# One layer of a hybrid attention trunk: a new order at the front, two weight sums on VectorE, a new place for the operands of two products, another term order in ff2, and other engines for the last rows

## The chip, the cores and the metric

The kernel runs on one core of one Trainium2 chip. The metric is the device time of one execution in microseconds (us), the median of several runs. Engines are named as the profile names them: PE (TensorE, matmuls), PEld (its weight loads), DVE (VectorE), ACT (ScalarE), POOL (GpSimd) and SP (SyncE, which issues DMAs here).

## The reference

Inputs are float32, the batch is 1, the sequence 512 rows, the model width 1024. RMSNorm divides a row by its root mean square and multiplies by a gain.

```python
u = rms_norm(h, g_mix)
z = u @ w_in                       # q, k, v of two attentions, forget logits, 2 x 1024 gates
y_a = sliding_window_attention(...) @ w_br_swa     # window 128, ALiBi, sinks
y_b = forgetting_attention(...) @ w_br_fox         # causal, decay bias from cumsum(log f)
mixed = sigmoid(gates[0]) * y_a + sigmoid(gates[1]) * y_b
h = h + mixed @ w_mix_out
u = rms_norm(h, g_mlp)
h = h + square(relu(u @ w_ff1)) @ w_ff2            # 1024 -> 4096 -> 1024
h = h + sigmoid(rms_norm(h, g_ple) @ w_ple_gate) * (p @ w_ple_proj)
out = rms_norm(h, g_final)
```

## The kernel before

**Three products for one.** Every matmul operand is kept as a high part (fp32r, cast by ACT) and a low part (what is left, subtracted by DVE). The helper `hi_lo` (L70 ACT, L71 DVE) splits activations; `emit_split` (L324 ACT, L325 DVE) splits weights into tiles named u0h, u0l, u1h and so on, the number counting the weight units in the order of use. A product is three matmuls: high by high, high by low, low by high. Four slots hold the high and four the low parts of weights, so a split waits until PE has ended the product that used the slot before.

**Rows.** The 512 rows are four blocks (tb) of 128. At the front each block is squared and summed (`square1`, DVE L435 for one half, ACT L432 for the other), POOL takes the root (L359, L362), DVE scales (`scale1`, L447), PE transposes in two halves of four 128x128 pieces (`to_uT`, L379), and `hi_lo` splits each half. The first products on it are those for v (`v_mm`, L467), for which `split_v` (L453, L454) splits eight blocks of weights.

**Seven products for eight.** ff1, ff2 and part of the gates use a scheme of the Strassen kind: a 2 x 2 block product is made from seven products of sums of blocks, numbered 1 to 7. ff1 products (`win_mm`, L910, 24 matmuls of 256 columns) are named ('f1', g) with the output bank x, y or z; ff2 products (`s2_mm`, L1309, 12 matmuls of 512 columns) are named s_. For ff1 the sums of activations are made once, in the mix stage (`put`), and kept split in `u2` and `at_ff`: products 1, 2, 4 and 6 have their operands in `u2`, one behind the other; the last three of them lie 48 words (`SHIFT`) off. For ff2, o is the squared ReLU of a product, split anew in each repetition. Sums of weights are made by `sum_source`: by an accumulating DMA that POOL issues (L298) or by DVE (L296).

**MLP in four repetitions.** The order within a repetition is a1 b1 a2 a5 b5 b2 a6 b6 a7 a3 b7 b3 A1 a4 b4 B1 A2 A5 B5 B2 A6 B6 A3 A7 B7 B3 A4 B4, with a, b ff1 of the even and the odd group, A, B ff2 of them. So products 1 of ff1 come directly behind the repetition before, and products 4 directly behind ff2's A1.

**What sets the order.** PE and POOL run in the order in which the code is written. ACT, DVE and SP are ordered by hand at the front, around the mix stage's end with the first steps of the first repetition, and in the last rows; elsewhere a scheduler orders them from dependencies and estimated times.

**The last rows.** `gate_piece` computes the last row block's gate in two pieces of 256 columns; `merge` (L1398 ACT, L1399 and L1400 DVE) applies a piece to h; `merge_ssq` (L1404 ACT) squares and sums it; POOL adds the sums (L1452) and takes the root (L1454); DVE and ACT scale (L1456 to L1462) and SP issues two stores (L1457, L1463).

## Time and profile before

| | before |
|---|---|
| median of 3 runs | 721.55 us (721.35 to 722.12) |
| the profiled execution's own time | 721.84 us |
| its span in the profile | 720.1 us |
| mean granted TensorE clock | 0.997 |
| one repetition of the MLP | about 77 us |

The span is what the profile sees of the execution; 1.74 us lie around it. A row of the timeline gives start and length in us, engine, line, operation, what it writes and reads, and in brackets how long the engine stood idle just before and what ended that. A row of the chain of waits gives start, length and what the time went to. A row of the stretches gives start:end, length, then busy time and count of instructions of PE, PEld, DVE, ACT and POOL, the granted clock, the DMA share and GB/s. Matmuls that follow each other without a stop overlap, so the pace is read from one start to the next, not from a row's length.

### The profile page before, as it was taken

To read this page: it belongs to the slowest core of one execution; us is meant where nothing else is said; L and a number is where in the kernel's file an instruction comes from. 1 tells how busy PE (TensorE), PEld (TensorE's weight loads), DVE (VectorE), ACT (ScalarE), POOL (GpSimd) and SP (SyncE) were. 2 spreads that over 40 slices of the span, in tenths; PEclk is the share of its full clock that TensorE was granted. 3 is DMA by queue.
4 is the path that set the end of the run, shared out by engine and by line. 5 is a ranking of instruction groups with operands and counts; after the bars stand their busy time and mean duration, and the time that the engine had idled before them with its cause. 6 is when DMAs were issued, how large, how long until landed. Compare 5 with 4: busy or idle time off the path is not lost.

```text
span 720.1 us, 11455 instructions
## 1 busy us (share of the span) xinstructions
PE 705.6 (98%) x4229; PEld 626.6 (87%) x4229; DVE 531.5 (74%) x900; ACT 449.4 (62%) x836; POOL 87.6 (12%) x127
## 2 busy tenths in 40 slices
PE   7999999999999999999999999999999999999995
PEld 6988888888888998888899789988999889988884
DVE  5567888877696556545879985899679966997564
ACT  5547888779863553344777646874578546866452
POOL 1011211100001200002410102010300020010101
PEclk9999999999999999999999999999999999999998
DMA  9256456670364894450995598739994689079002
GB/s 290 65 155 159 109 136 154 150 197 1 118 206 116 152 339 162 160 173 11 252 220 202 105 285 168 235 87 254 190 259 113 157 234 227 31 147 349 1 30 87
DMA packets 74055, 116.72 MB, mean 162 GB/s; under 512 B 6664, under 2 KB 44048, under 8 KB 74000
## 3 DMA queue, kind: packets, MB, share of 16 engines
q1 hardware_dynamic: 65792, 86.38, 37.9%
q0 software_dynamic: 8064, 29.36, 22.2%
q8 instruction: 33, 0.54, 0.3%
q10 hardware_dynamic: 144, 0.26, 0.1%
q14 instruction: 22, 0.18, 0.1%
HBM read 72.93 MB, written 4.19 MB: 107 GB/s over the span
## 4 chain that ended last, share of the span: by engine, by line
PE 85%; DVE 9%; ACT 2%; issue 2%; DMA 1%; POOL 0%; POOLq 0%; DVEq 0%; ACTq 0%
PE pf L74 5%; PE pf L76 5%; PE pf L75 5%; PE s_6x L1309 3%; PE s_4x L1309 3%; PE s_0x L1309 3%; PE s_2x L1309 3%; PE h_sc L752 2%; PE h_pv L822 2%; PE h_tr L810 2%; PE psy L75 2%; PE psy L76 2%; PE psy L74 2%; PE psm L76 2%; PE psm L75 2%; PE psm L74 2%
## 5 line engine op out<-in xcount | busy, mean ns | idle before, releaser
L298 POOL DMA_DIRECT2D wq<-wq x26 | 23.6, 942 | 174.9 <-DVE u154l L325 25.9
L770 ACT ACTIVATE s<-s,h_nm 128x128 f32<-128x128 f32 (+1 forms) x64 | 32.6, 512 | 5.9 <-DVE h_nm L763 5.1
L359 POOL TENSOR_SCALAR n_ms<-acc 128x1 f32<-128x1 f32 x15 | 6.3, 419 | 164.8 <-ACT junk L1075 100.4
L71 DVE TENSOR_TENSOR h_ptl<-h_tr,h_pth 128x512 fp32r<-128x512 f32 (+2 forms) x40 | 22.9, 604 | 3.9 <-ACT h_pth L70 3.6
L467 PE MATMUL va<-wv_h,u 128*128 128x320 f32 x64 | 20.1, 319 | 0.8 <-ACT u L70 0.7
L70 ACT CAST h_pth<-h_tr 128x512 fp32r<-128x512 f32 (+2 forms) x40 | 19.4, 523 | 1.8 <-PE h_tr L810 1.4
L70 ACT CAST u<-n_tr 128x512 fp32r<-128x512 f32 x22 | 12.2, 586 | 13.1 <-PE n_tr L1123 5.9
L810 PE MATMUL h_tr<-ident,s 128*128 128x128 f32 x136 | 19.6, 277 | 0.2
L467 PE MATMUL vb<-wv_h,u 128*128 128x328 f32 x64 | 19.6, 313 | 0.0
L298 POOL DMA_DIRECT2D wgw<-wgw x8 | 7.1, 970 | 101.9 <-DVE u25l L325 77.7
L71 DVE TENSOR_TENSOR u<-n_tr,u 128x512 fp32r<-128x512 f32 x22 | 14.6, 685 | 6.5 <-ACT u L70 6.5
L1075 ACT ACTIVATE junk<-h_sb 128x512 f32<-128x512 f32 x16 | 10.1, 630 | 12.3 <-DVE h_sb L1065 9.8
L822 PE MATMUL h_pv<-h_pth,v 128*128 128x256 f32 (+1 forms) x64 | 17.3, 291 | 0.0
L822 PE MATMUL h_pv<-h_ptl,v 128*128 128x256 f32 (+1 forms) x64 | 16.9, 305 | 0.3 <-DVE h_ptl L71 0.3
L810 PEld LDWEIGHTS h_tr<-ident,s 128*128 128x128 f32 x136 | 15.0, 141 | 2.0 <-ACT s L790 0.5
L1399 DVE TENSOR_TENSOR sgp<-sgp,pp 128x512 f32<-128x512 f32 (+1 forms) x9 | 5.7, 633 | 14.6 <-ACT sgp L1398 14.6
L1065 DVE TENSOR_TENSOR h_sb<-psm,h_sb 128x512 f32<-128x512 f32 x8 | 5.5, 689 | 14.3 <-PE psm L76 14.3
L790 ACT ACTIVATE s<-s,h_rec 128x128 f32<-128x128 f32 (+2 forms) x32 | 14.2, 482 | 2.3 <-DVE h_rec L784 2.3
L832 DVE TENSOR_TENSOR h_ao<-h_pv,h_ao 64x512 f32<-64x512 f32 x16 | 10.9, 681 | 6.1 <-ACT h_ao L831 5.8
L758 DVE CUSTOM_DVE_ANT_0 s<-h_sc,causal 128x128 f32<-128x128 f32 (+3 forms) x32 | 13.8, 482 | 0.3 <-PE h_sc L752 0.3
L784 DVE RECIPROCAL h_rec<-h_den 128x4 f32<-128x4 f32 x16 | 3.0, 185 | 14.5 <-ACT s L770 14.3
L822 PEld LDWEIGHTS h_pv<-h_ptl,v 128*128 128x128 f32 x64 | 12.1, 188 | 1.7 <-DVE h_ptl L71 0.8
(1607 smaller groups left out, 2773.8 us busy)
## 6 DMA issues: line engine op xcount, KB each, us to landing
wq<-in_w_ff_dram SPq DMA_DIRECT2D x45, 512.0 KB, 5.7
wq<-wq POOLq DMA_DIRECT2D x26, 512.0 KB, 5.1
wq_c<-in_w_ff_dram SPq DMA_DIRECT2D x9, 512.0 KB, 5.8
wg<-in_w_in_dram SPq DMA_DIRECT2D x4, 1024.0 KB, 5.4
wgw<-in_w_in_dram SPq DMA_DIRECT2D x8, 512.0 KB, 5.2
wgw<-wgw POOLq DMA_DIRECT2D x8, 512.0 KB, 5.8
wmix<-in_w_mix_out_dram SPq DMA_DIRECT2D x4, 1024.0 KB, 4.9
wpg<-in_w_ple_gate_dram SPq DMA_DIRECT2D x4, 1024.0 KB, 8.6
```

The source lines that it names most:

```text
L70: nc.scalar.copy(hi, src)
L71: nc.vector.tensor_tensor(lo, src, hi.bitcast(F32), ALU.subtract)
L74: nc.tensor.matmul(ps, lh, rh, start=start, stop=False)
L75: nc.tensor.matmul(ps, lh, rl, start=False, stop=False)
L76: nc.tensor.matmul(ps, ll, rh, start=False, stop=stop)
L298: nc.gpsimd.dma_start(q, other, accum_op=ALU.add)
L467: nc.tensor.matmul(ps, u[:, kk_, ts_], w[:, kk_, c0:c1], start=kk_ == 0 and n == 0, stop=kk_ == KT - 1 and n == 2)
L752: nc.tensor.matmul(ps[:, off:off + n], qs[i][z][:, qb * P:(qb + 1) * P], kk[i][z][:, k0:k0 + n], start=z == 0, stop=z == 1)
L770: nc.scalar.activation(sl, sl, AF.Exp, bias=nm[:, qb:qb + 1], accum_out=den[:, qb:qb + 1])
L810: nc.tensor.transpose(tr[:, n, :], c["s"][:, o, :], ident)
L822: nc.tensor.matmul(pv[:, q0:q0 + nq, :], V2[kb][:, c["v"], :], t[:, o:o + nq, :], start=n == 0, stop=n == 2 * NT - 1, skip_group_check=True)
L1309: nc.tensor.matmul(ps, o[:, j, ts_], w[:, j, :], start=tg != "" and j == 0 and n == 0, stop=j == 1 and n == 2, skip_group_check=True)
```

## The change

**Front.** `to_uT` is cut in two: `to_uT_pe` (transposes) and `to_uT_split`. Both halves of row block 0 are transposed before the first v product; the split of the second half and the square of row block 1 now stand ahead of the splits of the fourth and later blocks of v's weights. DVE, from the second half of row block 0's scaling on: wv_l are the low parts of v's weight blocks, u_80 the transposed rows, n_1_xn row block 1. Before:

```order
L454 TENSOR_TENSOR wv_l<-wv_108,wv_h 128x648
L71 TENSOR_TENSOR u_80<-n_0_tr_177,u_80 128x4x128
L454 TENSOR_TENSOR wv_l<-wv_108,wv_h 128x648
L454 TENSOR_TENSOR wv_l<-wv_111,wv_h 128x648 x2
L71 TENSOR_TENSOR u_80<-n_0_tr_204,u_80 128x4x128
L435 ISA n_1_xn,acc_1_223<-x_114 128x512
L435 ISA acc_1_223 128x1
L454 TENSOR_TENSOR wv_l<-wv_117,wv_h 128x648 x2
L447 SCALAR_TENSOR_TENSOR n_1_xn<-x_114,n_1_rs,g_ps_152 128x512
```

The same place of DVE after the change:

```order
L461 TENSOR_TENSOR wv_l<-wv_108,wv_h 128x648
L71 TENSOR_TENSOR u_80<-n_0_tr_175,u_80 128x4x128
L461 TENSOR_TENSOR wv_l<-wv_108,wv_h 128x648
L461 TENSOR_TENSOR wv_l<-wv_111,wv_h 128x648
L71 TENSOR_TENSOR u_80<-n_0_tr_180,u_80 128x4x128
L442 ISA n_1_xn,acc_1_209<-x_114 128x512
L442 ISA acc_1_209 128x1
L461 TENSOR_TENSOR wv_l<-wv_111,wv_h 128x648
L461 TENSOR_TENSOR wv_l<-wv_117,wv_h 128x648 x2
L454 SCALAR_TENSOR_TENSOR n_1_xn<-x_114,n_1_rs,g_ps_152 128x512
```

The fourth weight block's subtraction moved from ahead of the second half's split to behind row block 1's square. ACT's casts move alike.

**Operand places.** In `u2`, the first quarter (k = 0) of the operands of products 1 and 4 now lies at the start of the tile, the other three quarters 48 words off; products 2 and 6 follow. `win_mm` takes k outside and j inside, so that the first six matmuls of a product use the first quarter. `put` writes the two parts with instructions of their own.

**Two weight sums.** Those of products 6 and 7 of group 1 in the first repetition are made by DVE. DVE there (u57 to u60 are weight units, o_0_1 an ff2 operand, at_ff the operand of product 3). Before:

```order
L1135 SCALAR_TENSOR_TENSOR at_ff<-u_s_3_3914,at_ff 128x4x128
L325 TENSOR_TENSOR u57l<-wq_3517,u57h 128x1024
L325 TENSOR_TENSOR u58l<-wq_3659,u58h 128x1024
L925 TENSOR_TENSOR u_('f1', 0)_3995<-('f1', 0)y,u_('f1', 0)_3995 128x512
L325 TENSOR_TENSOR u59l<-wq_t_3495,u59h 128x1024
L1291 TENSOR_TENSOR o_0_1_4068<-u_('f1', 0)_3995,o_0_1_4068 128x512
L325 TENSOR_TENSOR u60l<-wq_3517,u60h 128x1024
```

After:

```order
L325 TENSOR_TENSOR u57l<-wq_3517,u57h 128x1024
L325 TENSOR_TENSOR u58l<-wq_3659,u58h 128x1024
L296 TENSOR_TENSOR wq_3517<-wq_3517,wq_3660 128x1024
L296 TENSOR_TENSOR wq_3518<-wq_3518,wq_3660 128x1024
L933 TENSOR_TENSOR u_('f1', 0)_4003<-('f1', 0)y,u_('f1', 0)_4003 128x512
L325 TENSOR_TENSOR u59l<-wq_t_3495,u59h 128x1024
L325 TENSOR_TENSOR u60l<-wq_3517,u60h 128x1024
L1312 TENSOR_TENSOR o_0_1_4076<-u_('f1', 0)_4003,o_0_1_4076 128x512
L1155 SCALAR_TENSOR_TENSOR at_ff<-u_s_3_3920,at_ff 128x4x128
```

Two sums stand ahead of the bank's addition, and one part of product 3's operand moved behind o_0_1. On ACT, a little earlier, the other part (L1154, at_ff from u_s_2) moved ahead of two copies (L1223, ppo) of the projection's results.

**ff2.** The matmuls that read the operand's upper part come first (four), the two with the lower part last; before, each of the two k pieces had upper, upper, lower.

**Last rows.** DVE squares, sums and adds the rest in one instruction (L1475); ACT scales the first 512 columns and issues their store; DVE scales the last two pieces. DVE there before and, behind it, after:

```order
L1399 TENSOR_TENSOR sgp_768_7432<-sgp_768_7432,pp_7052 128x256
L1400 TENSOR_TENSOR h_sb<-h_sb,sgp_768_7432 128x256
L1456 TENSOR_SCALAR o_7365<-o_7365,n_l_rs 128x512
L1458 SCALAR_TENSOR_TENSOR o_7365<-h_sb,n_l_rs,g_final_bc 128x256
L1462 TENSOR_TENSOR o_7365<-sgp_768_7432,g_final_bc 128x256
```

After:

```order
L1471 TENSOR_TENSOR o_7373<-h_sb,g_final_bc 128x256
L1420 TENSOR_TENSOR sgp_768_7441<-sgp_768_7441,pp_7060 128x256
L1421 TENSOR_TENSOR h_sb<-h_sb,sgp_768_7441 128x256
L1475 ISA sgp_768_7441,n_l_ms<-h_sb,acc_3_564 128x256
L1475 ISA n_l_ms 128x1
L1482 TENSOR_SCALAR o_7373<-o_7373,n_l_rs 128x256
L1483 SCALAR_TENSOR_TENSOR o_7373<-h_sb,n_l_rs,g_final_bc 128x256
```

The scaling of 512 columns left DVE, and the square came to it.

The diff:

```diff
         else:
             q = quadrant(i, 0, pn == 7)
             other = quadrant(i, *{5: (0, 1), 7: (1, 1), 6: (1, 1), 4: (1, 0)}[pn])
-            if key[0] == "s2" and pn in (5, 7):
+            if key[0] == "s2" and pn in (5, 7) or key in (("f1", 1, 6), ("f1", 1, 7)):
                 nc.vector.tensor_tensor(q, q, other, ALU.add)
             else:
                 nc.gpsimd.dma_start(q, other, accum_op=ALU.add)
...
                                            ALU.mult)
         return xn
-    def to_uT(xn, uh, ul, tb, trp, name, tg="tr", halves=(0, 1)):
-
-        for half in halves:
-            tr = trp.tile([P, 4, P], F32, tag=tg, bufs=3, name=f"{name}_tr{half}")
-            for j in range(4):
-                k = half * 4 + j
-                nc.tensor.transpose(tr[:, j, :], xn[:, k * P:(k + 1) * P], ident)
-            sl = (slice(None), slice(half * 4, half * 4 + 4), slice(tb * P, (tb + 1) * P))
-            hi_lo(uh[sl], ul[sl], tr)
+    def to_uT_pe(xn, trp, name, half, tg="tr"):
+
+        tr = trp.tile([P, 4, P], F32, tag=tg, bufs=3, name=f"{name}_tr{half}")
+        for j in range(4):
+            k = half * 4 + j
+            nc.tensor.transpose(tr[:, j, :], xn[:, k * P:(k + 1) * P], ident)
+        return tr
+
+    def to_uT_split(tr, uh, ul, tb, half):
+        sl = (slice(None), slice(half * 4, half * 4 + 4), slice(tb * P, (tb + 1) * P))
+        hi_lo(uh[sl], ul[sl], tr)
+
+    def to_uT(xn, uh, ul, tb, trp, name, tg="tr"):
+
+        for half in range(2):
+            to_uT_split(to_uT_pe(xn, trp, name, half, tg), uh, ul, tb, half)
     def new_uT(name):
         t = up.tile([P, 2 * KT * S + SHIFT], F32R, tag="u", bufs=1, name=name)
...
             gps.append(ps)
         warm_up(N_WARM[2])
         scale1(0, square1(0))
+        trs0 = [to_uT_pe(xn1[0], psA, "n1_0", half) for half in range(2)]
         split_v(0)
-        to_uT(xn1[0], uh, ul, 0, psA, "n1_0", halves=(0,))
+        to_uT_split(trs0[0], uh, ul, 0, 0)
+        split_v(1)
         v_mm(0, 0)
-        for k in (1, 2, 3):
-            split_v(k)
-            if k == 1:
-                v_mm(0, 1)
-        to_uT(xn1[0], uh, ul, 0, psA, "n1_0", halves=(1,))
+        v_mm(0, 1)
+        split_v(2)
+        to_uT_split(trs0[1], uh, ul, 0, 1)
+        acc = square1(1)
+        split_v(3)
         v_mm(0, 2)
         v_mm(0, 3)
-        acc = square1(1)
         split_v(4)
         split_v(5)
         scale1(1, acc)
...
             bank[key, bk] = mm_tile(f"{key}{bk}", tg).rearrange("q (j s) -> q j s", j=2)
         ps = bank[key, bk]
         wh, wl = unit(key + (pn,))
-        oh, ol = op
-        for j in range(2):
-            for k in range(4):
+        oh, ol = ([t[:, k] for t in o for k in range(t.shape[1])] for o in op)
+        for k in range(4):
+            for j in range(2):
                 for n, (w, o) in enumerate(((wh, oh), (wh, ol), (wl, oh))):
-                    nc.tensor.matmul(ps[:, j, :], w[:, k, j, :], o[:, k, :],
+                    nc.tensor.matmul(ps[:, j, :], w[:, k, j, :], o[k],
                                      start=tg != "" and j == 0 and k == 0 and n == 0,
                                      stop=k == 3 and n == 2, skip_group_check=True)
...
     u2, u_op = new_uT("u2"), {}
-    for n, pn in enumerate((1, 2, 4, 6)):
-        o = 2048 * n + (SHIFT if n else 0)
-        u_op[pn] = [u2[:, o + 1024 * e:o + 1024 * e + 1024].rearrange("q (k s) -> q k s", k=4)
+    n2 = 1024 + SHIFT
+    for n, pn in enumerate((1, 4)):
+        first = [u2[:, 512 * n + 256 * e:512 * n + 256 * e + 256].rearrange("q (k s) -> q k s", k=1)
+                 for e in range(2)]
+        rest = [u2[:, n2 + 768 * e:n2 + 768 * e + 768].rearrange("q (k s) -> q k s", k=3)
+                for e in range(2)]
+        u_op[pn] = [list(t) for t in zip(first, rest)]
+        n2 += 1536
+    for pn in (2, 6):
+        u_op[pn] = [[u2[:, n2 + 1024 * e:n2 + 1024 * e + 1024].rearrange("q (k s) -> q k s", k=4)]
                     for e in range(2)]
+        n2 += 2048
     at_ff = at_pool.tile([P, 6144 + SHIFT], F32R, tag="c", name="at_ff")
...
                            **dict(zip(names[:-1], shape[1:-1])))
     def new_op(pn):
-        u_op[pn] = [spare(c, f"u2_{pn}{'hl'[i]}", (P, 4, 256))
+        u_op[pn] = [[spare(c, f"u2_{pn}{'hl'[i]}", (P, 4, 256))]
                     for i, c in enumerate({5: (0, 1), 7: (2, 3), 3: (4, 5)}[pn])]
...
     def put(pn, tb, src):
         sl = t2_cols(tb)
-        hi, lo = u_op[pn][0][sl], u_op[pn][1][sl]
-        if pn != 3:
-            hi_lo(hi, lo, src)
-            return
-        nc.scalar.mul(hi, src, -1.0)
-        nc.vector.scalar_tensor_tensor(lo, src, -1.0, hi.bitcast(F32), ALU.mult, ALU.subtract)
+        k = 0
+        for hi, lo in zip(*u_op[pn]):
+            n = hi.shape[1]
+            hi, lo, part = hi[sl], lo[sl], src[:, k:k + n]
+            k += n
+            if pn != 3:
+                hi_lo(hi, lo, part)
+                continue
+            nc.scalar.mul(hi, part, -1.0)
+            nc.vector.scalar_tensor_tensor(lo, part, -1.0, hi.bitcast(F32), ALU.mult,
+                                           ALU.subtract)
     def t2_top(tb):
...
                 bank[g // 2, "2" + bk, i] = mm_tile(f"s2_{g}{bk}{i}", tg)
             ps = bank[g // 2, "2" + bk, i]
             ts_ = slice(i * P, i * P + P)
-            for j in range(2):
-                for n, (o, w) in enumerate(((oh, wh), (oh, wl), (ol, wh))):
-                    nc.tensor.matmul(ps, o[:, j, ts_], w[:, j, :],
-                                     start=tg != "" and j == 0 and n == 0,
-                                     stop=j == 1 and n == 2, skip_group_check=True)
+            terms = [(o[:, j, ts_], w[:, j, :]) for o, ws in ((oh, (wh, wl)), (ol, (wh,)))
+                     for j in range(2) for w in ws]
+            for n, (o, w) in enumerate(terms):
+                nc.tensor.matmul(ps, o, w, start=tg != "" and n == 0, stop=n == 5,
+                                 skip_group_check=True)
     def s2_out(fq, pn):
...
         merge_ssq(LT, sg, 512, 256, 1)
         finish(LT - 1)
         acc = acc4[LT]
-        nc.vector.tensor_tensor(acc[:, 0:1], acc[:, 0:1], acc[:, 1:2], ALU.add)
+        nc.vector.scalar_tensor_tensor(acc[:, 0:1], acc[:, 0:1], EPS, acc[:, 1:2], ALU.add,
+                                       ALU.add)
+        nc.vector.tensor_tensor(o[:, 512:768], h_sb[:, LT, 512:768], gb4[:, 512:768], ALU.mult)
         sg = merge(LT, ps1, 768, 256)
-        merge_ssq(LT, sg, 768, 256, 2)
+        hl = h_sb[:, LT, 768:1024]
         ms = sm.tile([P, 1], F32, tag="ms", name="n4_l_ms")
-        nc.gpsimd.tensor_scalar(ms, acc[:, 0:1], acc[:, 2:3], EPS, ALU.add, ALU.add)
+        nc.vector.tensor_tensor_reduce(sg[:, 256:512], hl, hl, 1.0 / D, acc[:, 0:1], ALU.mult,
+                                       ALU.add, ms)
         rs = sm.tile([P, 1], F32, tag="rs", name="n4_l_rs")
         nc.gpsimd.tensor_tensor(rs, ms, mhalf, ALU.pow)
         rows_ = slice(LT * P, (LT + 1) * P)
-        nc.vector.tensor_scalar(o[:, 0:512], o[:, 0:512], rs, None, ALU.mult)
-        nc.sync.dma_start(out[rows_, 0:512], o[:, 0:512])
-        nc.vector.scalar_tensor_tensor(o[:, 512:768], h_sb[:, LT, 512:768], rs, gb4[:, 512:768],
-                                       ALU.mult, ALU.mult)
-        hg = sg[:, 256:512]
-        nc.scalar.activation(hg, h_sb[:, LT, 768:1024], AF.Copy, scale=rs)
-        nc.vector.tensor_tensor(o[:, 768:1024], hg, gb4[:, 768:1024], ALU.mult)
+        nc.scalar.mul(o[:, 0:512], o[:, 0:512], rs)
+        nc.scalar.dma_start(out[rows_, 0:512], o[:, 0:512])
+        nc.vector.tensor_scalar(o[:, 512:768], o[:, 512:768], rs, None, ALU.mult)
+        nc.vector.scalar_tensor_tensor(o[:, 768:1024], hl, rs, gb4[:, 768:1024], ALU.mult,
+                                       ALU.mult)
         nc.sync.dma_start(out[rows_, 512:1024], o[:, 512:1024])
```

More of the change, by code (lines that the diff above doesn't have):

```diff
@@ L1036, in layer_kernel @@
         else:
-            win_mm(t[:3], t[3], g_op[t[3]], {})
+            win_mm(t[:3], t[3], [[o] for o in g_op[t[3]]], {})
         done = t
```

## The prediction

> **What bounds the kernel now.** I read the page first (busy shares, then the chain that ended last), then the waits of PE alone, then the chain and the timeline at the places that the change touches.
>
> ```profile
> PE 705.6 (98%) x4229; PEld 626.6 (87%) x4229; DVE 531.5 (74%) x900; ACT 449.4 (62%) x836; POOL 87.6 (12%) x127
> PE 85%; DVE 9%; ACT 2%; issue 2%; DMA 1%; POOL 0%; POOLq 0%; DVEq 0%; ACTq 0%
> ```
>
> The first row gives busy time by engine, the second the shares of the chain. TensorE is busy for 98% and carries 85% of the chain. So an edit saves time in three ways only: it makes matmuls follow each other faster, it takes away a place where PE stands still, or it shortens what lies behind the last matmul. The waits of PE, by what ended them:
>
> ```profile
> PE n_tr L379 <- DVE n_xn L447: 1.1, 2, 0.6
> PE s_0z L1309 <- DVE o L71: 0.7, 1, 0.7
> PE ('f1', 0)x L910 <- ACT u_('f1', 0)_4203 L921: 0.7, 1, 0.7
> ```
>
> Columns: total, times, longest, in us. Three of the five edits stand at these waits. The other two concern the pace of ff1's matmuls and the last rows.
>
> **Part 1, the front.** The chain of waits there, and with it the DVE and ACT rows ahead of it and PE's wait in between:
>
> ```profile
> 8.99 0.41 PE L467 MATMUL va<-wv_h,u 128*128 128x320 f32 x1 [0.68 <-ACT u L70]
> 8.83 2.00 ACT L453 CAST wv_h<-wv 128x648 fp32r<-128x648 f32 x3
> 9.60 2.32 DVE L454 TENSOR_TENSOR wv_l<-wv,wv_h 128x648 fp32r<-128x648 f32 x3
> 12.45 0.69 DVE L71 TENSOR_TENSOR u<-n_tr,u 128x512 fp32r<-128x512 f32 x1 [0.52 <-ACT u L70]
> 13.06 0.68 DVE n_xn L435
> 13.69 1.58 DVE L454 TENSOR_TENSOR wv_l<-wv,wv_h 128x648 fp32r<-128x648 f32 x2
> 13.91 1.45 POOL n_ms L359
> 15.44 0.58 POOL n_rs L362
> 16.04 0.76 DVE n_xn L447
> 16.93 0.64 PE n_tr L379 x4
> ```
>
> Row block 1's transposes (16.93) wait for its scaling (16.04), that for POOL's two steps, those for the square at 13.06, and that stands behind the split of the second transposed half (12.45), whose transposes PE does only between v products. The change lets PE transpose that half directly after the first, inside its 0.68 idle at 8.3 to 9.0; the extra 0.3 us that may show there is paid back where the transposes stood. ACT then does two weight casts (2 x 0.67 from 8.83) and the half's cast by about 10.8; DVE two subtractions (2 x 0.77 from 9.60, so 11.15), the half's subtraction, 0.6, and the square ends at 12.4 instead of 13.74. POOL's delay from the square's end to the scaling was 16.04 - 13.74 = 2.30, which gives 14.7. DVE must also pass the subtractions moved behind the square: 12.4 + 0.77 + 1.58 = 14.75, or a little more if a weight block lands late. The scaling starts at about 14.85, 1.2 earlier; PE has its own v products to finish first, so I take 1.1. Nothing behind it on PE waits until long after, so the gain stays. Bounds: 0.6 (the weight blocks hold DVE for another 0.5) and 1.3 (the whole advance of the square). The casts moved on ACT delay only wv's later blocks, whose products PE reaches after the transposes.
>
> **Part 2, ff1's products 1 and 4.** Three stretches of 48 or 240 matmuls of 256 columns each, start:end, length, then the busy times: the two products 1 of the second repetition, the ten products behind them, the two products 4; and PE rows just at the first border:
>
> ```profile
> 432.41:438.16 5.75, 5.75 (x49) 5.74 (x48) 3.44 (x4) 2.58 (x3) 1.75 (x2) 1.00 0.57 108
> 438.16:465.38 27.22, 27.22 (x242) 27.22 (x241) 18.99 (x20) 20.17 (x28) 3.47 (x4) 1.00 0.93 226
> 468.12:473.77 5.65, 5.65 (x49) 5.64 (x48) 5.65 (x7) 4.43 (x7) 0.00 (x0) 1.00 0.26 85
> 438.17 0.40 PE L910 MATMUL ('f1', 2)y<-u,u83h 128*128 128x256 f32 x2
> 438.53 0.39 PE L910 MATMUL ('f1', 2)y<-u,u83h 128*128 128x256 f32 x2
> 438.87 0.39 PE L910 MATMUL ('f1', 2)y<-u,u83h 128*128 128x256 f32 x2
> ```
>
> The stretches give 119.8, 113.4 and 117.7 ns for a matmul of the same shape, with a granted clock of 1.00. The matmuls of product 1 are those whose operand's address and the address of the weights loaded beside it differ by a multiple of 128 words; in the ten others, and in product 4, the distance is off by 48 words. Product 4 follows directly on ff2 matmuls of 512 columns and never reaches the pace of the ten. Behind product 1, product 2 needs three matmuls to reach it (0.36 us for the first three, 0.34 for the next). After the change one quarter of the operand of products 1 and 4 (6 of 24 matmuls) lies at the slow distance, done first, and 18 at the other. If the pace behaves as at 438.17, a product takes 8 matmuls at 120, one at 116, 15 at 113.4: 2.78 us, and the pair 5.55. Product 1 gains 5.75 - 5.55 = 0.20 and 0.02 at product 2's start; product 4 gains 5.65 - 5.55 = 0.10. Over four repetitions: 4 x 0.32 = 1.3. Bounds: 0 (distance doesn't set the pace) and 2.0 (all but the six at 113.4: 4 x (0.27 + 0.02 + 0.17) = 1.84, rounded up for product 2).
>
> The Trainium skill ("TensorE: Matmul & The Clock Gate", section "Step-by-step: what each phase is for") says that the streamed operand and the weight load have two independent read ports, and that loading the next weights takes no read bandwidth from the running matmul. By that rule the placement would change nothing and this term would be 0. The rows at 432.41 and 438.16 speak against it, but only as a correlation.
>
> The new places also cut the operand's splits into a quarter and three quarters: 4 more instructions on ACT and 4 on DVE, in the mix stage, where the last transposes wait for DVE and ACT. An extra piece costs at most a 128x512 split's difference in overhead; I take 0.15 off (0 to 0.3).
>
> **Part 3, two weight sums.** POOL's accumulating DMAs of (f1,1,6) and (f1,1,7), ACT behind them, PE's wait, and a sum that DVE does already:
>
> ```profile
> 363.02 1.76 POOL L298 DMA_DIRECT2D wq<-wq  x2 [3.80 <-DVE u57l L325]
> 369.13 1.05 ACT L324 CAST u60h<-wq 128x1024 fp32r<-128x1024 f32 x1 [2.35 <-DMA wq<-wq]
> 375.70 0.28 PE L910 MATMUL ('f1', 1)x<-u,u60l 128*128 128x256 f32 x1
> 376.65 0.50 PE L910 MATMUL ('f1', 0)x<-at_ff,u61h 128*128 128x256 f32 x2 [0.68 <-ACT u_('f1', 0)_4203 L921]
> 376.02 0.58 ACT L921 COPY u_('f1', 0)_4203<-('f1', 0)x 128x512 f32<-128x512 f32 x1
> 381.92 1.23 DVE L296 TENSOR_TENSOR wq<-wq,wq_gb 128x1024 f32<-128x1024 f32 x1
> ```
>
> ACT stands 2.35 us for the DMA (363.02 to 369.13, 6.1); its later casts run back to back, so the copy of the product bank comes late, and PE stops from 375.81 (one pitch after 375.70) to 376.65, 0.84, and starts again slowly (0.34 for two matmuls instead of 0.23): 0.95 in all. On DVE the two sums cost 2 x 1.23 = 2.46. They stand behind the same splits that POOL waited for, so they run from about 363.5 to 366, ahead of the bank add that ACT's next steps read, and of the weight splits, all of which slip by that much; ACT then still casts u60h at about 364.7 instead of 369.13. The last cast ahead of the copy waits for its weight slot, free when PE ends the product before, at 375.81 - 24 x 0.1134 = 373.1; cast and copy end at 373.1 + 1.05 + 0.58 = 374.7, ahead of the 375.8 at which PE wants the bank. I take the whole 0.95 (bounds 0 and 0.95). The scheduler also puts the split for product 3 ahead of the projection's copies on ACT, where it waits for PE and POOL; I see about 1 us of room there before PE needs a bank, so 0, and up to 0.6 if the room is less.
>
> **Part 4, ff2's order.** PE and DVE at product 5 of the odd group, first and second repetition:
>
> ```profile
> 404.43 0.39 PE L1309 MATMUL s_0z<-u71l,o 128*128 128x512 f32 x1
> 405.51 0.73 PE L1309 MATMUL s_0z<-u71h,o 128*128 128x512 f32 x2 [0.69 <-DVE o L71]
> 404.77 0.68 DVE L71 TENSOR_TENSOR o<-z_('f1', 1)_4130,o 128x512 fp32r<-128x512 f32 x1
> 481.94 0.39 PE L1309 MATMUL s_2z<-u99h,o 128*128 128x512 f32 x1
> 482.16 0.39 PE L1309 MATMUL s_2z<-u99l,o 128*128 128x512 f32 x1
> 482.69 0.73 PE L1309 MATMUL s_2z<-u99h,o 128*128 128x512 f32 x2
> 483.27 0.39 PE L1309 MATMUL s_2z<-u99l,o 128*128 128x512 f32 x1
> ```
>
> The third matmul needs the operand's lower part, which DVE delivers last. Matmuls of 512 columns follow each other in 0.227 us; at 482.16 the next comes after 0.53, so 0.30 are lost, and the two behind it take 0.58 instead of 0.454, another 0.11. In the new order the lower part is needed at the fifth matmul, 2 x 0.227 = 0.454 later, more than the wait. So 0.41 is gained in each of the last three repetitions, which the trace shows alike: 1.24. In the first the loss is 405.51 - 404.43 - 0.227 = 0.853 and 0.11. There the new order gives back 0.454; parts 2 and 3 bring PE there earlier by about 1.2, and DVE, freed of its wait for ACT, by about as much, so half a microsecond of waiting stays: 0.45. Bounds for both: 0, if DVE, which now also has the two sums, falls behind by what PE wins, and 2.2.
>
> **Part 5, the last rows.** What follows the last matmul:
>
> ```profile
> 713.12 0.52 ACT sgp L1404 x2
> 713.73 0.30 POOL n_l_ms L1452
> 714.07 0.61 POOLq L1488
> 714.71 0.48 DVE o L1456
> 715.22 0.33 SPq L1457 DMA_DIRECT2D out_dram<-o  x1
> 715.95 0.33 SPq L1463 DMA_DIRECT2D out_dram<-o  x1
> ```
>
> The square and sum on ACT and POOL's addition (713.12 to 714.03) become one DVE step of 256 columns. The like step of 512 columns took 0.68 at 13.06, so about 0.5, and the root is there 0.4 earlier. Then ACT scales the first 512 columns and issues their store on its own queue, while DVE scales 2 x 256 columns (0.39 + 0.42 by the chain's pace at 714.71): SP's store goes at about 715.05 instead of 715.95, 0.9 earlier. But the two stores, 0.73 apart before, now go together, and may delay each other; I give that 0.3. Gain 0.6 (0.2 to 0.95). The added multiplication on DVE lies in the wait for the last sigmoid.
>
> **Sum.** 1.1 + 1.3 - 0.15 + 0.95 + 1.24 + 0.45 + 0.6 = 5.5 off the profiled execution's 721.84: 716.35. The runs' median of before, 721.55, lies 0.29 under it, so I forecast 716.1. About 0.2%, 1.4 us, is what a measurement of this kernel can tell from no change; faster means under 720.1.
>
> **Rivals.**
> - *The distance doesn't matter.* Then part 2 gives nothing: 717.4. For it: product 4 is slow at the good distance too (117.7). Against it: 119.8 and 113.4 with nothing else different. The skill's rule of the two ports, named above, would have it so. 0.13.
> - *DVE stays what ff2 waits for.* DVE takes 2.46 us of sums and more pieces, and the 0.3 and 0.85 waits move with it; part 4's 1.69 is lost: 717.8. Against it: the last three repetitions are far from the added work. 0.12.
> - *ACT's early place for product 3's split holds the stage.* ACT waits for PE and POOL ahead of a copy that frees a bank for PE; 0.6 of stall and part of part 3: 716.9 to 717.5. 0.1.
> - *The other side: the slow quarter sets the pace of all of ff1.* Product 4 keeps 117.7 over 48 matmuls, so a pace once slow can last. If six slow matmuls at the head of a product keep the ten products behind them at 120 too, these 240 matmuls cost 6.6 ns more each, 4 x 240 x 6.6 ns = 6.3 us, part 2's 1.3 is lost, and the time is 723.7. It decides from the point where two thirds of them stay slow. Against it: product 2 leaves 120 after three matmuls, at 438.17. 0.04.
>
> **How the numbers follow.** The forecast's case has 0.58, the rivals 0.13, 0.12, 0.1 and 0.04, unnamed trouble 0.03. The likeliest case alone runs from 714.7 (the better ends of parts 1, 2 and 5 and no loss in the mix stage: 0.2 + 0.7 + 0.35 + 0.15 less) to 717.1 (the worse ends of parts 1 and 5 and of the mix stage: 0.5 + 0.4 + 0.15 more). The range keeps the low end and takes in the first three rivals with 0.3 to spare: 714.7 to 718.1. Faster has the forecast's case and the first three rivals, 0.93, less 0.01 for two of them coming together; same has that and the unnamed, 0.04; slower has the last rival, 0.04.
>
> **What would show it.** In the trace after: row block 1's transposes at about 15.8 instead of 16.93; the stretches of products 1 and 4 at 5.55 each, with only the first eight matmuls of a product at 120; no idle time of PE ahead of u61h's matmuls and no POOL DMA at 363; no gap in product 5 in the last three repetitions and about 0.45 in the first; the last store about 0.9 earlier against the last matmul. It would be wrong if PE shows a new wait in the mix stage between 345 and 360, if product 2 and those behind it run at 120, or if the store's time grows by what its issue gains.

## The result and the profile after

| | before | changed |
|---|---|---|
| median | 721.58 us (721.35 to 722.12, 4 runs) | 717.09 us (716.72 to 719.09, 4 runs) |
| profiled execution | 721.84 us, span 720.1 | 717.04 us, span 715.3 |

The ratio is 0.9943 (95% interval 0.9931 to 0.9955): 4.5 us faster by the medians, 4.8 by the profiled executions, where 5.5 was forecast. The page of the changed kernel, busy time by engine, and the two rows of PE's waits that lie in the changed parts:

```profile
PE 704.0 (98%) x4229; PEld 625.7 (87%) x4229; DVE 533.6 (75%) x908; ACT 450.2 (63%) x838; POOL 84.9 (12%) x124
PE va L474 <- DVE wv_l L461: 0.6, 1, 0.6
PE n_tr L1139 <- DVE n_xn L369: 0.4, 1, 0.4
```

PE is as bound as before. The three waits named in the prediction are gone; two smaller ones, at the front and in the mix stage, are new. The three stretches of the second repetition, as shown of before:

```profile
429.88:435.41 5.53, 5.53 (x50) 5.53 (x48) 3.02 (x4) 2.59 (x3) 1.75 (x2) 1.00 0.38 73
435.41:462.61 27.20, 27.20 (x243) 27.20 (x241) 19.05 (x21) 19.91 (x28) 3.48 (x4) 1.00 0.97 237
465.34:470.87 5.53, 5.53 (x49) 5.53 (x48) 5.53 (x7) 4.69 (x7) 0.00 (x0) 1.00 0.32 92
```

Products 1 fell from 5.75 to 5.53, products 4 from 5.65 to 5.53; the ten products between kept 27.2. The weight sums: DVE, ACT and the first matmuls that had waited:

```profile
362.96 2.36 DVE L296 TENSOR_TENSOR wq<-wq,wq 128x1024 f32<-128x1024 f32 x2
364.44 1.05 ACT L324 CAST u60h<-wq 128x1024 fp32r<-128x1024 f32 x1 [1.38 <-PE ('f1', 0)z L918]
375.23 0.39 PE L918 MATMUL ('f1', 0)x<-at_ff,u61h 128*128 128x256 f32 x2
```

ACT casts u60h 4.7 us earlier than before, and u61h's matmuls follow without a gap (no bracket). Product 5 of ff2's odd group, first and second repetition:

```profile
403.24 0.39 PE L1331 MATMUL s_0z<-u71l,o 128*128 128x512 f32 x1
403.46 0.92 PE L1331 MATMUL s_0z<-u71h,o 128*128 128x512 f32 x3
479.73 0.39 PE L1331 MATMUL s_2z<-u99l,o 128*128 128x512 f32 x1
480.18 0.98 PE L1331 MATMUL s_2z<-u99h,o 128*128 128x512 f32 x3
```

In the first the fifth matmul follows at the usual 0.22: the whole wait went. In the second it follows after 0.45, so 0.23 of a wait is left; the last experiment shows that this wait belongs to one execution. Start times of the same matmuls in both traces, subtracted, give this account of PE (plus is time lost):

| stage | us | forecast |
|---|---|---|
| front, up to the mix stage | -0.83 | -1.1 |
| mix stage, ahead of the last transposes | +0.49 | +0.15 |
| ff1's products 1 and 4 | -1.39 | -1.3 |
| stall at the weight sums | -0.97 | -0.95 |
| ff2's product 5, four repetitions | -0.89, -0.05, -0.35, -0.40 | -0.45, -0.41, -0.41, -0.41 |
| gate stage | +0.11 | 0 |
| from the start of the last matmul to the end | -0.6 (8.8 to 8.2) | -0.6 |

### The profile page after: what moved, and what is told of

Its sections match the earlier page's. It is cut to its first block, busy times and chain, and to the rows that moved or that the text cites. A ratio compares the mean times of both kernels' runs of the same rounds, so it can differ in the third digit from the quotient of the medians.

```text
span 715.3 us, 11463 instructions
## 1 busy us (share of the span) xinstructions
PE 704.0 (98%) x4229; PEld 625.7 (87%) x4229; DVE 533.6 (75%) x908; ACT 450.2 (63%) x838; POOL 84.9 (12%) x124
## 4 chain that ended last, share of the span: by engine, by line
PE 90%; DVE 4%; issue 2%; ACT 1%; DMA 1%; POOL 0%; SPq 0%; POOLq 0%; DVEq 0%; ACTq 0%
PE pf L76 5%; PE pf L74 5%; PE pf L75 5%; PE s_6x L1331 3%; PE s_4x L1331 3%; PE s_0x L1331 3%; PE s_2x L1331 3%; PE h_sc L760 3%; PE h_pv L830 2%; PE h_tr L818 2%; PE psy L75 2%; PE psy L76 2%; PE psy L74 2%; PE va L474 2%; PE vb L474 2%
## 5 line engine op out<-in xcount | busy, mean ns | idle before, releaser
L298 POOL DMA_DIRECT2D wq<-wq x24 | 21.8, 936 | 165.3 <-DVE u70l L325 25.9
L70 ACT CAST u<-n_tr 128x512 fp32r<-128x512 f32 (+2 forms) x26 | 12.6, 519 | 12.2 <-PE n_tr L1139 5.6
L71 DVE TENSOR_TENSOR u<-n_tr,u 128x512 fp32r<-128x512 f32 (+2 forms) x26 | 15.0, 603 | 5.8 <-ACT u L70 5.7
```

Source lines behind the costliest of these rows:

```text
L70: nc.scalar.copy(hi, src)
L71: nc.vector.tensor_tensor(lo, src, hi.bitcast(F32), ALU.subtract)
L298: nc.gpsimd.dma_start(q, other, accum_op=ALU.add)
```

## The experiments

All are the changed kernel with one edit, or with two where that is said; medians stand beside its 717.09.

**The places of before, with the new loop order.**

```diff
-        u_op[pn] = [list(t) for t in zip(first, rest)]     # products 1, 4: a quarter at 0, rest 48 off
+        o = 2048 * n + (SHIFT if n else 0)                 # 1, 2, 4, 6 in one piece each
```

> The changed kernel with the operands of products 1 and 4 back in their places of before (one piece each, product 1 at a multiple of 128 words from the weights), but with the new loop order, k outside. Theory (the distance sets the pace, and the two pieces cost 0.45 us of PE wait in the mix stage): the pairs of products 1 and 4 go back to 5.75 and 5.65 us, in sum 1.3 us over four repetitions; PE's wait of 0.44 ahead of the last transposes of the mix stage goes; about 0.9 us slower than the changed kernel. Rival (the loop order makes the pace): the pairs stay at 5.53, and the kernel is 0.45 us faster than the changed one.

717.46 us (716.89 to 719.00). The stretches of the second repetition:

```profile
430.00:435.75 5.75, 5.75 (x50) 5.75 (x48) 3.35 (x4) 2.59 (x3) 1.75 (x2) 1.00 0.60 114
435.75:462.97 27.22, 27.22 (x243) 27.22 (x241) 19.08 (x21) 20.18 (x28) 3.47 (x4) 1.00 0.93 227
465.70:471.36 5.66, 5.66 (x50) 5.65 (x48) 5.66 (x7) 4.42 (x7) 0.00 (x0) 1.00 0.27 87
```

Both pairs are back at 5.75 and 5.65, so the places make the pace and not the loop order. (This edit, like the next ones on the pace, moves the operand and leaves the weights where they are. So no run tells whether it is the distance to the weights that counts or the operand's own address.) The mix stage's wait is gone: PE gains 0.49 against the changed kernel at the last transposes. The products then cost 1.3 over four repetitions, as expected, but 0.4 of it comes back at product 5 of the second repetition, where PE, now later, no longer waits. The net is 0.4, not the 0.9 expected, and the medians (0.37 apart) don't separate the kernels.

**All operands 48 words off, none at a multiple of 128.**

```diff
+        o = 2048 * n + SHIFT
```

> The changed kernel with all operands of products 1, 2, 4 and 6 in one piece each and 48 words off the multiple of 128, none at a multiple. Theory (behind 512-column matmuls the pace at 48 words stays at 117.7 ns until some matmuls at a multiple of 128 reset it, so the slow quarter does work): the pairs of products 1 and of products 4 both take 5.65, the products 2 behind products 1 stay slow too until something resets them; 1.0 us lost, 0.45 won back in the mix stage, 0.5 us or more slower than the changed kernel. Rival (only the distance counts, and product 4 is slow for a reason of its own): product 1 at 113.4 ns, 5.44 a pair, product 4 at 5.65; about 0.35 us faster than the changed kernel.

720.65 us (720.53 to 720.97), 3.6 slower than the changed kernel.

```profile
430.13:435.78 5.65, 5.65 (x50) 5.65 (x48) 3.17 (x4) 2.58 (x3) 1.75 (x2) 1.00 0.56 107
435.78:464.05 28.27, 28.27 (x243) 28.27 (x242) 19.59 (x22) 20.51 (x29) 3.48 (x4) 1.00 0.90 223
466.77:472.42 5.65, 5.65 (x50) 5.65 (x48) 5.65 (x7) 4.14 (x6) 0.00 (x0) 1.00 0.24 80
```

Every product of ff1 runs at 117.8 ns, the ten between too (28.27 / 240), in all four repetitions. The theory was right, and its "0.5 us or more" became 3.6. So 48 words have two paces, 117.8 and 113.3, and which one holds depends on what ran before: behind ff2's 512-column matmuls it is 117.8 and stays, behind a run of matmuls at a multiple of 128 it is 113.3 and stays. The slow quarter is what makes the rest fast. That explains product 4 before the change, the row that had spoken for the first rival.

**Fewer slow matmuls: 2 of 24, then 4 of 24.** The low, then the high part alone of the first quarter lies at a multiple of 128. The order of the split changes too: in the first kernel ACT casts an operand in one piece, in the second its two casts come ahead of DVE's subtractions. In both, PE's wait of 0.44 in the mix stage is gone.

```diff
+        u_op[pn] = [[hi], [lo0, lo1]]      # 2 of 24: matmuls 2 and 5
+        u_op[pn] = [[hi0, hi1], [lo]]      # 4 of 24: matmuls 1, 3, 4 and 6
```

> The changed kernel with only the low part of the first quarter of products 1 and 4 at a multiple of 128 words: 2 of 24 matmuls, the second and the fifth, instead of the first 6; ACT casts an operand in one piece, DVE subtracts it in two. Theory (each slow matmul shifts the two read streams against each other, and few are enough to leave the 117.8 pace): the pairs of products 1 and 4 fall from 5.53 to 5.46 to 5.50, all other products of ff1 stay at 113.3, and the mix stage's wait of 0.44 falls by 0.2 or more; 0.4 to 0.8 us faster than the changed kernel. Rival (a run of several slow matmuls is needed): all products of ff1 stay at 117.8, as with all operands 48 words off, 3 us slower than the changed kernel.

> The changed kernel with only the high part of the first quarter of products 1 and 4 at a multiple of 128 words: 4 of a product's first 6 matmuls (first, third, fourth, sixth), with ACT's two casts ahead of DVE's two subtractions. Theory (each slow matmul moves the streams a little, two isolated ones are too few, six in a row are enough): four of six are enough, all products behind them run at 113.3, pairs of products 1 and 4 at 5.50 to 5.55, mix-stage wait under 0.15: 0.3 to 0.4 us faster than the changed kernel, like the grouped pieces. Rival (the slow ones must follow each other): 117.8 in most of ff1 as with the low quarter, 2.5 us slower than the changed kernel.

719.55 us (719.16 to 719.79) and 717.22 us (716.61 to 717.68). Second repetition, the low part's stretches first:

```profile
429.40:435.05 5.65, 5.65 (x49) 5.65 (x48) 3.29 (x4) 2.59 (x3) 1.75 (x2) 1.00 0.58 111
435.05:463.32 28.27, 28.27 (x243) 28.27 (x241) 19.47 (x22) 20.53 (x29) 3.48 (x4) 1.00 0.91 223
466.04:471.69 5.65, 5.65 (x49) 5.65 (x48) 5.65 (x7) 4.15 (x6) 0.00 (x0) 1.00 0.23 80
```

```profile
429.03:434.63 5.60, 5.60 (x50) 5.60 (x48) 3.06 (x4) 2.59 (x3) 1.75 (x2) 1.00 0.57 109
434.63:461.83 27.20, 27.20 (x243) 27.20 (x241) 19.38 (x21) 20.18 (x28) 3.46 (x4) 1.00 0.95 228
464.56:470.16 5.60, 5.60 (x49) 5.59 (x48) 5.60 (x7) 4.43 (x7) 0.00 (x0) 1.00 0.28 89
```

Two of 24 don't change the pace (only in the first repetition, where the mix stage runs ahead, they did). With four, the first product stays at 117.7 ns a matmul and the second, with the next four, ends at 113: it takes more than four scattered slow matmuls, and six in a row are enough. My expectation missed for two. For four it was half right: the products behind ran at 113.3, but the pairs took 5.60 instead of 5.50 to 5.55, and the kernel wasn't faster than the changed one. Both expectations speak of two read streams that are shifted against each other; no run shows that. In the third repetition of the kernel with four, the pace also fell back: from u117h on, behind a stop of 0.04, four products ran at 117.8. That cost this execution about 0.4 us (4 x 24 x 4.5 ns).

**Other offsets: 16 and 32 words.**

```diff
+        o = 2048 * n + 16        # and, in the second kernel, 32; products 5, 7, 3 stay at 48
```

> The changed kernel with the operands of products 1, 2, 4 and 6 in one piece each, 16 words off the multiple of 128 instead of 48; those of products 5, 7 and 3 stay at 48. Theory (a pace is kept until a run of matmuls at another distance changes it; 48 words keep 117.8 when it is entered behind 512-column matmuls): at 16 words the streams meet otherwise; if 16 words have a pace of their own, products 1, 2, 6 and 4 all show one value, and products 5, 7 and 3, at 48, keep 117.8 or 113.3 depending on it. Rival (117.8 is simply the pace behind 512-column matmuls at any distance but a multiple of 128): all ff1 products at 117.8, 3.5 us slower than the changed kernel.

> As the run at 16 words, at 32 words. Same theories; if either offset gives 113.3 for products 1 and 4 without any matmul at a multiple of 128, the kernel is 1.2 us faster than the changed one (8 products at 2.72 instead of 2.77 us, 0.4, and the mix stage's 0.45, and no slow matmuls behind); if it keeps 117.8 or 120, 3.5 us or more slower.

720.25 us (719.79 to 720.34) and 719.79 us (719.27 to 720.02). Products 1, 2, 4 and 6 run at 117.8 ns at 16 words and at 118.4 to 120.0 at 32. Behind products at 32 words, products 5, 7 and 3 (at 48) run at 113.3; behind those at 16 words they do in the first repetition and stay at 117.8 in the second. So the rival's 117.8 holds at 16 words but for the first repetition (3.2 us slower than the changed kernel), and at 32 words the pace is another. No offset tried gives the fast pace behind 512-column matmuls by itself.

**The pieces in another order.** The loss in the mix stage. ACT, DVE and PE in the changed kernel:

```profile
340.59 0.27 ACT L70 CAST u<-n_tr 128x128 fp32r<-128x128 f32 x1 [0.76 <-DVE u_s L1171]
340.89 0.29 DVE L71 TENSOR_TENSOR u<-n_tr,u 128x128 fp32r<-128x128 f32 x1 [0.33 <-ACT u L70]
341.22 0.48 ACT L70 CAST u<-n_tr 128x384 fp32r<-128x384 f32 x1 [0.36 <-DVE u L71]
341.73 0.56 DVE L71 TENSOR_TENSOR u<-n_tr,u 128x384 fp32r<-128x384 f32 x1 [0.55 <-ACT u L70]
342.21 0.68 DVE L1073 TENSOR_TENSOR h_sb<-psm,h_sb 128x512 f32<-128x512 f32 x1
345.97 0.39 PE L76 MATMUL pspp<-at_ff 128*128 128x512 f32 x1
346.80 1.29 PE L1139 MATMUL n_tr<-ident,n_xn 128*128 128x128 f32 x8 [0.44 <-DVE n_xn L369]
```

ACT's second cast waits for DVE's first subtraction (its bracket), so the four steps run in turn. DVE's addition to h queues behind them, and with it the scaling for which PE's last transposes wait. In before, PE came from the last matmul to the transposes without such a wait:

```profile
346.80 0.39 PE L76 MATMUL pspp<-at_ff 128*128 128x512 f32 x1
347.14 1.29 PE L1123 MATMUL n_tr<-ident,n_xn 128*128 128x128 f32 x8
```

```diff
-                hi_lo(hi, lo, part)          # cast, subtract, cast, subtract
+                nc.scalar.copy(hi, part)     # both casts, then both subtractions
```

> The changed kernel with the operand's two pieces split in another order: ACT's two casts first, then DVE's two subtractions. Theory (the loss in the mix stage is ACT and DVE waiting for each other in turn): DVE's addition to h behind the split of row block 2 comes 0.3 us earlier, PE's wait ahead of the last transposes falls from 0.44 to 0.15 or less, and the kernel is 0.3 us faster than the changed one. Rival (the pieces' own length makes the loss): the wait stays at 0.35 or more and the time is the same within 0.1.

716.84 us (716.66 to 717.17), ratio to before 0.9932 (0.9918 to 0.9947).

```profile
340.55 0.65 ACT L1153 CAST u<-n_tr 128x128 fp32r<-128x128 f32 x2 [0.76 <-DVE u_s L1179]
341.23 0.76 DVE L1156 TENSOR_TENSOR u<-n_tr,u 128x128 fp32r<-128x128 f32 x2 [0.71 <-ACT u L1153]
341.91 0.68 DVE L1073 TENSOR_TENSOR h_sb<-psm,h_sb 128x512 f32<-128x512 f32 x1
346.05 0.39 PE L76 MATMUL pspp<-at_ff 128*128 128x512 f32 x1
346.50 1.18 PE L1139 MATMUL n_tr<-ident,n_xn 128*128 128x128 f32 x7
```

The step from PE's last matmul to the transposes is 0.45, against 0.83 in the changed kernel and 0.34 in before: 0.38 of the 0.49 lost is back, and it was the waiting in turn. The kernel's median is only 0.25 lower, inside the spread. In this trace PE's lead over the changed kernel grows by 0.29 at product 5 of the second repetition (the last experiment says why) and shrinks by 0.45 in the gate stage. ACT waits there for the ple gate's first weights, which it casts at 655.90 instead of 656.06, though their load was issued at 644.38 instead of 644.97. The wait for this load differs from trace to trace, 1.28 to 2.14 us in all.

**The front's order of before.**

```diff
-        trs0 = [to_uT_pe(xn1[0], psA, "n1_0", half) for half in range(2)]
+        # transposes of half 1 behind v_mm(0, 1); square1(1) behind split_v(3)
```

> The changed kernel with the order of before at the front, all else changed. Theory (the front's order brings the transposes of row block 1 forward by 0.65, and PE's lead of 0.8 lasts until the mix stage, where 0.45 of it is lost in the wait for DVE): row block 1's transposes at 16.9 us; PE at the end of the mix stage later by only 0.35, so 0.35 us slower than the changed kernel if the mix stage's wait is set by DVE's own chain, 0.8 if that chain moves with PE. Rival (the front's gain is only the landing of a weight block in one execution): no difference beyond 0.2.

718.53 us (718.14 to 719.64), 1.4 slower, more than either figure expected. The first cast of v's weights and the transposes, changed kernel and then this one; the last row is the first cast in before:

```profile
7.85 0.73 ACT L460 CAST wv_h<-wv 128x648 fp32r<-128x648 f32 x1 [3.11 <-DMA wv<-in_w_in_dram]
16.28 1.17 PE L378 MATMUL n_tr<-ident,n_xn 128*128 128x128 f32 x8
```

```profile
8.07 0.73 ACT L460 CAST wv_h<-wv 128x648 fp32r<-128x648 f32 x1 [3.33 <-DMA wv<-in_w_in_dram]
17.50 1.29 PE L378 MATMUL n_tr<-ident,n_xn 128*128 128x128 f32 x8 [0.60 <-DVE n_xn L454]
```

```profile
7.25 0.73 ACT L453 CAST wv_h<-wv 128x648 fp32r<-128x648 f32 x1 [2.35 <-DMA wv<-in_w_in_dram]
```

The transposes are 1.22 later, and PE is still 1.31 later at the last transposes of the mix stage; the wait there is the same 0.44, so it doesn't come from PE's lead, as I had thought, and DVE's chain moves with PE. Later 0.30 comes back at product 5 of the second repetition and 0.58 is lost in the gate stage, where ACT's wait for the load named above is 2.14 instead of 1.57. The landing of v's first weights varies: the cast ran at 7.25 in before's profile and at 6.83 to 7.90 in the eleven executions with the new order. There the transposes came at 15.72 to 16.53, the middle one at 15.99; with the old order at 16.93 and 17.50. The middle one and the mean of the old order's two are 1.2 apart. The two pairs of executions with the nearest landing (casts at 7.25 and 7.34, at 8.07 and 7.90) are 0.97 apart each. So the front is worth 1.0 to 1.2 by these rows. The 0.65 between the two profiles shown above is less, at least in part because the weights landed 0.6 earlier in before's.

**The weight sums by POOL again.**

```diff
-            if key[0] == "s2" and pn in (5, 7) or key in (("f1", 1, 6), ("f1", 1, 7)):
+            if key[0] == "s2" and pn in (5, 7):
```

> The changed kernel with the two weight sums of the first repetition made by POOL's accumulating DMA again. Theory (PE waits for the copy behind ACT, which waits for that DMA): PE stands about 0.85 ahead of u61h's products and starts slowly by 0.1; PE then comes later to ff2's product 5, where DVE is no longer late, so nothing is given back: 0.9 us slower than the changed kernel. Rival (the sums on DVE cost as much at a later place as they save): the same within 0.2.

718.61 us (717.89 to 721.85), 1.5 slower where 0.9 was expected.

```profile
376.02 0.50 PE L918 MATMUL ('f1', 0)x<-at_ff,u61h 128*128 128x256 f32 x2 [0.94 <-ACT u_('f1', 0)_4211 L929]
```

The wait is back and 0.26 longer than the 0.68 of before, since PE came earlier; with the slow start PE loses 1.23 there, by the starts of the matmuls.

**ff2's order of before.**

```diff
-            terms = [... for o, ws in ((oh, (wh, wl)), (ol, (wh,))) for j in range(2) for w in ws]
+            terms = [... for j in range(2) for o, w in ((oh, wh), (oh, wl), (ol, wh))]
```

> The changed kernel with ff2's terms in the order of before. Theory (the lower part of the operand is late by less than the 0.454 us that the new order gives): PE waits come back at product 5 of the odd group, 0.9 in the first repetition, 0.4 in each of the third and fourth and 0.3 to 0.7 in the second, where the changed kernel still waits 0.2; 1.7 us (1.4 to 2.2) slower than the changed kernel. Rival (other edits already made DVE early enough): under 0.5.

718.33 us (718.09 to 718.77), 1.2 slower, under the 1.4 to 2.2 expected; by the starts of the matmuls the four places cost 0.45, 0.20, 0.46 and 0.51 against the changed kernel, 1.6 in all, and the front of this execution was 0.2 earlier. The last of them:

```profile
634.23 0.74 PE L1331 MATMUL s_6z<-u155h,o 128*128 128x512 f32 x2 [0.25 <-DVE o L71]
```

In the first repetition the old order costs only 0.45 now, where 0.9 was expected. The third matmul there stands 0.42 behind its usual time, against 0.85 in before, so the other half of the 0.89 gained there comes from the other edits, with which DVE is earlier against PE.

**The last rows of before.**

```diff
-        nc.scalar.mul(o[:, 0:512], o[:, 0:512], rs)
-        nc.scalar.dma_start(out[rows_, 0:512], o[:, 0:512])
+        nc.vector.tensor_scalar(o[:, 0:512], o[:, 0:512], rs, None, ALU.mult)
+        nc.sync.dma_start(out[rows_, 0:512], o[:, 0:512])
```

> The changed kernel with the last rows of before. Theory: from the last matmul to the last store's issue 0.95 longer, but the two stores 0.7 apart land faster; span from the last matmul's end to the end 0.5 longer; 0.5 us slower than the changed kernel. Rival (two stores at once cost what the earlier issue gains): the same within 0.2.

717.33 us (716.80 to 717.49). The issues of the last two stores, in the changed kernel on ACT's and SP's queue, here on SP's; the last matmul starts at 707.06 and 707.09:

```profile
710.77 0.38 ACTq L1481 DMA_DIRECT2D out_dram<-o  x1
710.79 0.33 SPq L1485 DMA_DIRECT2D out_dram<-o  x1
```

```profile
710.99 0.33 SPq L1478 DMA_DIRECT2D out_dram<-o  x1
711.72 0.33 SPq L1484 DMA_DIRECT2D out_dram<-o  x1
```

The last issue is 0.90 earlier in the changed kernel, and the stores land 2.6 and 2.7 after their issue instead of 2.0 and 2.1: the two at once take back 0.6 of the 0.9. From the last matmul to the end: 8.2 against 8.63, so 0.43; the medians are too near to show it.

**Pieces cast first, and the fourth weight block ahead of the square.**

```diff
-        acc = square1(1)
         split_v(3)
+        acc = square1(1)
```

> The changed kernel with the operand pieces cast first and subtracted behind (as in the run with grouped pieces) and with the fourth weight block's split ahead of row block 1's square at the front. Theory: PE's wait of 0.63 for that split ahead of v's products goes, the square comes 0.75 later but POOL's root is still there when DVE ends the sixth weight block, so the transposes come 0.1 to 0.3 earlier; with the 0.3 of the grouped pieces 0.4 to 0.6 us faster than the changed kernel. Rival (the later square delays the scaling): no gain from the front, 0.3 faster in all.

These are two edits; the diff shows the one at the front. 717.41 us (716.88 to 719.83, 6 runs): no gain. The wait for that block went, but the scaling then waited 0.77 for POOL and PE 0.58 for the scaling: the rival was right about the front. Its 0.3 in all did not show either: the 0.38 gained in the mix stage was lost again, 0.26 of it in the second repetition. PE and DVE of this kernel there, then DVE of the changed kernel, then DVE and PE of the kernel with the pieces cast first alone:

```profile
480.17 0.96 PE L1339 MATMUL s_2z<-u99h,o 128*128 128x512 f32 x3 [0.35 <-DVE o L71]
460.61 1.23 DVE L296 TENSOR_TENSOR wq_c<-wq_c,wq 128x1024 f32<-128x1024 f32 x1 [0.47 <-DMA wq<-in_w_ff_dram]
```

```profile
460.61 1.23 DVE L296 TENSOR_TENSOR wq_c<-wq_c,wq 128x1024 f32<-128x1024 f32 x1 [0.18 <-DMA wq<-in_w_ff_dram]
```

```profile
460.05 1.22 DVE L296 TENSOR_TENSOR wq_c<-wq_c,wq 128x1024 f32<-128x1024 f32 x1
479.65 0.92 PE L1339 MATMUL s_2z<-u99h,o 128*128 128x512 f32 x3
```

In the first two DVE stands until the same 460.61 for a weight load, although PE and DVE were 0.3 earlier in the one, and works without a stop from there to the lower part that product 5 waits for. In the third the load was there in time, and the fifth matmul, at 479.65, follows without a wait. The same holds over all twelve traces with ff2's new order: these two alone have DVE standing for that load, and these two alone have a late fifth matmul in the second repetition; in the ten others it follows at 0.23. So the 0.23 of wait left in the changed kernel's trace, and with it about 0.3 of the 0.36 by which the second repetition fell short of its forecast, come from a late load in that execution. No run moved the load on purpose.

## Why the prediction came out as it did

- **Front.** Right in mechanism and size: 1.1 forecast, 1.0 to 1.2 by the executions with either order. The transposes came at 15.99 in the middle one of eleven, not at 15.8; PE waits 0.6 for the fourth weight block behind the square, a wait that I did not see coming.
- **Products 1 and 4.** Right to 0.1, and the shape too: the pairs at 5.53 where 5.55 was said. The reason given was half of it. I took the distance to set the pace and the rest to be a short run-in; the runs show a pace that is kept, and slow matmuls that switch it. Products 4 ran at 117.7 at the good distance, and nothing in my working said why a slow quarter should make the rest of them faster: that part of the number came from the likeness to the row at 438.17 alone, and that it held was luck. The upper bound was also summed wrongly: with six slow matmuls in each of the two products a pair takes 5.52, which gives 4 x (0.23 + 0.02 + 0.13) = 1.5 and not 1.84. And "nothing else different" in the first rival was too much said: what ran ahead was different too. The rival that placement doesn't matter is refuted by the kernel with the old places. The rival on the other side, a pace that lasts, was right that it lasts and wrong in which way six slow matmuls turn it. The same 48 matmuls took 5.75, 5.65 or 5.53 us by place and history alone, and this term measured 1.4. The Trainium skill ("TensorE: Matmul & The Clock Gate", section "Step-by-step: what each phase is for") says that loading the next weights takes no read bandwidth from the running matmul. By that rule the placement would have changed nothing, which these times speak against; but whether the weight load is the other party here no run shows, since the weights never moved.
- **Mix stage.** The step that failed: "An extra piece costs at most a 128x512 split's difference in overhead". The new pieces cost 0.49, over the upper bound of 0.3. Of that 0.38 came back with the other order of the same pieces, because ACT's second cast waited for DVE's first subtraction. The look should have gone to who waits for whom between the pieces, not to their lengths.
- **Weight sums.** 0.95 forecast, 0.97 measured, by the path that was named. The earlier split for product 3 cost nothing, as assumed.
- **ff2.** The sum, 1.69, was met (1.69), but in part by luck, since its parts were not: 0.9 in the first repetition, where half a microsecond of waiting was expected to stay, and nearly nothing in the second, where 0.23 of waiting and a slow restart stayed because a weight load was late in that execution.
- **Last rows.** 0.6 forecast, 0.43 to 0.6 measured: the issue gained the 0.9 said, but the two stores cost each other 0.6 and not 0.3.
- **Sum.** Of the 0.7 missing in the profiled execution, 0.3 are the mix stage and 0.3 the front, where v's weights landed later than in before's execution; the rest is small. The kernel is 1 us over the forecast, inside the range.

## What to carry to other kernels

Read the pace of a stream of equal matmuls from start to start over whole products; a few percent between streams of one shape are worth a search in the places of the operands, and the stream ahead is part of the cause. When an operand is cut in two, write all steps of one engine ahead of the other engine's, or the two engines wait in turn. Undo one part at a time: two gains of this change were partly eaten by its own side costs, which the total alone would not have told. And look at one place in all traces before giving a wait a cause: at product 5 of the second repetition ten traces showed what one could not.

## What the runs showed of the hardware

- Matmuls of 128x256 with a granted clock of 1.00 follow each other in 113.3, 117.8 or 120 ns. With the operand a multiple of 128 words from the weights it is 120; with 48 words it is 117.8 behind 512-column matmuls and 113.3 behind six matmuls of the former kind; each of the two was kept over 240 matmuls and more. In the first repetition less was enough for 113.3: two of the former kind, or products at 16 words ahead. What inside the chip keeps the state was not measured, nor whether the distance to the weights or the operand's own address counts.
- The fast pace fell back to the slow one once, at a stop of PE of 0.04 (0.153 from start to start instead of 0.113) ahead of u117h, in the kernel with four slow matmuls:

```profile
527.37 0.28 PE L918 MATMUL ('f1', 5)x<-u,u116l 128*128 128x256 f32 x1
527.52 0.50 PE L918 MATMUL ('f1', 4)x<-at_ff,u117h 128*128 128x256 f32 x2
```

u117 and the three products behind it ran at 117.8. Longer stops did not do so: 0.12 at the same place and 0.94 at 376.02 in the kernel with POOL's sums, and 0.33 at the same place in the kernel with the last rows of before. So what made the pace fall is open.
- Two 256 KB stores issued together on ACT's and SP's queues landed after 2.6 to 2.7 us, and 2.0 to 2.1 when issued 0.73 apart on SP's.
